# A second column page for the pair jobs, wider spaced taps, diagonal zeroing and a thinner filler in the scan

## The chip, the cores and the metric

The kernel runs on one core of one Trainium2 chip. Its time is the device time of one execution in microseconds (us); a kernel's time is the median of its runs. The engines are TensorE (PE, matmuls, with PEld for its weight loads), VectorE (DVE), ScalarE (ACT), GpSimd (POOL) and SyncE (SP), which here only issues transfers. POOL issues transfers too, among them those that add what they bring to what lies in the target.

## The reference

One layer of a hybrid encoder over 1024 positions of width 1024, in float32. Cut to what matters here:

```python
h  = rmsnorm(x)
P  = h @ W_in          # columns for: GLU of the convolution, q, v, z_fwd, z_bwd, out gate, gA, gB
A  = pointwise(swish(layernorm(dwconv31(glu(P)))))          # depthwise, 31 taps, 512 columns
B  = out_proj(norm(bi_hgrn2(q, v, z_fwd, z_bwd)) * swish(og))  # gated scan, 8 heads, both directions
x  = x + W_out(sigmoid(gA) * A + sigmoid(gB) * B)
x  = x + W_down(silu(dwconv3(h2 @ W_gate)) * (h2 @ W_up))    # h2 = rmsnorm(x)
out = rmsnorm(x)
```

The scan of one head is S_t = diag(f_t) S_{t-1} + k_t v_t^T, o_t = S_t^T q_t, forward and backward.

## The kernel before

Every number is held as a high and a low part, and every product is three matmuls (`mm3`, L147 to L149: high by high, high by low, low by high). Splitting a weight page into its two parts is a cast on ACT and a subtraction on DVE (`split`, L123). PE's instructions are issued in the order of the program; on the other engines and the transfer queues the framework orders them. Work for PE is written as generators that stop at every piece of some matmuls, and a `Stream` takes so many pieces as `fill(n)` tells it, carrying fractions (and what is overdrawn) over in `owed`.

The stages, in order of time: the first norm and the GLU jobs; then 19 pair jobs for the rest of W_in's columns; then some projection jobs; then the scan of the eight heads; its tail; the output projections, the merge, the feed-forward part and the last norm.

**Pair jobs** (`pair_job`, `in_pair`). Two blocks of 128 columns are made by a scheme of seven products instead of eight, so that sums of weight quadrants are needed. One pair has 14 pieces of six matmuls. `steps` prepares the weights of a pair: a page of rows ("wr", two buffers, `raw_w`), a page of columns ("sw", one buffer, filled by two loads of 256 KB, L304 and L305), to which src1 is added; `sums` then adds the columns to the rows and the rows to themselves. `add` does an addition on DVE where `first` holds (L296), and elsewhere with a transfer that adds, issued by POOL (L300). With `first`, src1 is loaded into a row page. Then rows are split into the weights 1 and 2, after the sums into 6 and 3, the columns into 7 and 5 ("wq"), and the last quadrant into 4. `first` holds for pair 0 and from pair 12 on. `evac` combines the products on DVE (L718) and stores them.

**Convolution** (`conv_steps`). Four column tiles, each with 31 taps on DVE (L953 the first, L956 the others), one tap at a time over 1024 positions; after each tile its two halves are stored to memory (L961). Between two taps the stream of pairs is filled:

```python
for _ in conv_steps():
    s_pairs.fill(CONV_FILL)
```

The LayerNorm then loads the tiles back half by half ("cx", L978) and adds them up (L968), with pieces of the pairs between its parts.

**Scan.** For each head and each of its two halves, `scan_levels` makes four steps (h = 8, 16, 32, 64) and `scan_states` three; each level multiplies the pages qF and kG by decays on DVE (L1061). At h = 32 a PSUM bank is zeroed by one matmul of a zero page `none` with itself (L1230), and `blocks` (L1207) writes the 32x32 and 64x64 blocks off the diagonal into it. At h = 64 the whole bank is copied to S_t, and then the 32x32 blocks on the diagonal are overwritten from D_t. After each of the 112 steps `between(FILL)` gives the stream `dense` (projections of what is left, pieces of six 128x512 matmuls) its FILL pieces, then a step of the next half's preparation, then one piece of the last head's outputs (`pending`).

**Tail** (after the loop). The last head's outputs (`outputs`: L1314, L1316, L1333, L1340) are stepped by hand between fills of `dense`, with the rest of `dense` drained at the end.

Of the kernel before, what the change touches and what calls it, by code (L numbers as in the profile page):

```python
# [10 lines left out]
F32 = mybir.dt.float32  # L11
# [5 lines left out]
AX = mybir.AxisListType  # L17

P = 128
FILL = 1.3  # L20
CONV_FILL = 1.6
NPAIRS = 19
LN_FILL = 6
LN_LAST = 12
# [6 lines left out]
H = 512  # L31
# [15 lines left out]
def tile_hybrid_encoder(  # L47
# [22 lines left out]
    nc = tc.nc  # L70
    PSUM = bass.MemoryType.PSUM
    V, A, G, T = nc.vector, nc.scalar, nc.gpsimd, nc.tensor

    S, D = x.shape[1], x.shape[2]
    ND = D // P
# [17 lines left out]
    def nm(s):  # L93
        uid[0] += 1
        return f"{s}_{uid[0]}"
# [36 lines left out]
    def raw_w(src, nk):  # L132
        t = mp.tile([P, nk, P], F32, tag="wr", name=nm("wr"), bufs=2)
        nc.sync.dma_start(t, src)
        return t
# [142 lines left out]

        return prep, run

    def pair_job(src0, src1, nk, acts, wpool, pool, evac, su=4, first=False, late=False, now=False, direct=False):

        def steps(w):
            def both(src, alt, late=late):  # L290
                hi, lo = split(w_page(2 * nk, alt), w_page(2 * nk, alt), src, V, late)
                return [(hi[:, :nk], lo[:, :nk]), (hi[:, nk:], lo[:, nk:])]

            def add(o, a):
                if first:
                    V.tensor_tensor(o, o, a, op=ALU.add)  # L296
                elif direct:
                    pin(V.tensor_tensor(o, o, a, op=ALU.add))
                else:
                    G.dma_start(o, a, accum_op=ALU.add)  # L300

            rows = raw_w(src0, 2 * nk)
            col = wpool.tile([P, 2 * nk, P], F32, tag="sw", name=nm("sw"), bufs=1)
            nc.sync.dma_start(col[:, :nk], src0[:, :nk])  # L304
            nc.sync.dma_start(col[:, nk:], src1[:, :nk])  # L305
            if not direct:
                add(col, raw_w(src1, 2 * nk) if first else src1)
            def sums():
                add(rows[:, :nk], col[:, nk:])
                add(rows[:, nk:], rows[:, :nk])  # L310

            def quadrant():
                a22 = pool.tile([P, nk, P], F32, tag="w4", name=nm("w4"), bufs=1)
                nc.sync.dma_start(a22, src1[:, nk:])
                return a22

            if now:
                w[1], w[2] = both(rows, None, False)
                sums()
                yield 0  # L320
                w[6], w[3] = both(rows, None, False)
                yield 1
                a22 = quadrant()
                yield 2
                w[7], w[5] = both(col, pool)
                yield 4
            elif direct:
                yield 2
                other = raw_w(src1, 2 * nk)
                yield 2  # L330
                w[1], w[2] = both(rows, None)
                a22 = quadrant()
                yield 6
                add(col, other)
                sums()
                yield 1
                w[6], w[3] = both(rows, None)
                yield 1
                w[7], w[5] = both(col, pool)
                yield 4  # L340
            else:
                yield 4
                w[1], w[2] = both(rows, None)
                sums()
                a22 = quadrant()
                yield 6
                w[7], w[5] = both(col, pool)
                yield 3
                w[6], w[3] = both(rows, None)
                yield 3  # L350
            one = w_page(2 * nk, pool)
            w[4] = split(one[:, :nk], one[:, nk:], a22, V, late)

        def prep():
            w = Weights(steps)
            return w if late else w.all()

        def run(w):
            def product(i, acc, fresh=True):
                for k in range(nk):  # L360
                    mm3(acc, w[i], acts(i)[k], k, fresh and k == 0, k == nk - 1, not fresh)
                    if k % 2 == 1 or k == nk - 1:
                        yield

            def copy(acc):
                t = page(pool, "su", su)
                A.copy(t, acc)  # L367
                return t

            row, b2, col = bank("mm"), bank("tr"), bank("sc")  # L370
            yield from product(1, row)
            p1 = copy(row)
            yield from product(2, b2)
            evac(0, 0, b2, p1, ALU.add)
            yield from product(6, row, False)
            u2 = copy(row)
            yield from product(7, col)
            p7 = copy(col)
            yield from product(5, row, False)
            evac(1, 1, p7, row, ALU.subtract)  # L380
            yield from product(4, col, False)
            evac(1, 0, col, u2, ALU.subtract)
            yield from product(3, row, False)
            evac(0, 1, row)

        return prep, run
# [113 lines left out]
    def in_cols(c0):  # L500
        return w_cols(w_in, 0, ND, c0)
# [206 lines left out]
    for j in range(NCW):  # L708
        g = gp0.tile([P, PAD + S + PAD], F32, tag="gl", name=nm("gl"), bufs=NCW)
# [38 lines left out]
    def in_pair(n):  # L748
        (c0, e0), (c1, e1) = todo[2 * n], todo[2 * n + 1]
        evs = (e0, e1)  # L750
        return pair_job(
            in_cols(c0),
            in_cols(c1),
            NK2,
            lambda i: ht[i],
            p1,
            p1,
            lambda e, *quadrant: evs[e](*quadrant),
            first=n == 0 or n >= 12,
        )  # L760

    gate = {}
# [200 lines left out]
    for _ in conv_steps():  # L963
        s_pairs.fill(CONV_FILL)

# [40 lines left out]
    rest = todo[2 * NPAIRS :]  # L1006
# [37 lines left out]
    dense = Stream(run_jobs(rest_jobs))  # L1044


    hp = tc.alloc_tile_pool(name="heads", bufs=1, reuse_waits="tile")
    NB = H // 8
    DE = hp.tile([P, 2, 2, H], F32, name="DE")
    dg = hp.tile([P, 4, 32], F32, name="dg")  # L1050
    none = hp.tile([P, H], mybir.dt.bfloat16, name="none")
    E0, D0 = 0, 2 * H
    for o in (E0 + 3, D0 + 3):
        G.memset(view(DE, o, [[8, 2 * NB]]), 1.0)
# [101 lines left out]
    def scan_levels(base, S_t, Tt):  # L1156
# [62 lines left out]
        b = bank("sc")  # L1219
        inside(b)  # L1220
        for h in (8, 16, 32, 64):
            n, nb = H // (2 * h), H // h
            if h < 32:
                if h == 16:
                    b = bank("ob")
                level(b, h)
            else:
                if h == 32:
                    b = bank("sc")
                    T.matmul(b, none[:, :P], none, start=True, stop=True)  # L1230
                blocks(b, h)
            tt(pairs(kG, h), pairs(kG, h), view(tb, 1, [[2, n], [nb - 1, 2], [0, h]]))
            tt(pairs(qF, h), pairs(qF, h), view(tb, nb + 1, [[2, n], [nb - 1, 2], [0, h]]))
            if h < 64:
                tn = hp.tile([P, 3, NB], F32, tag="tb", name=nm("tb"), bufs=3)
                k = 3
                to = view(tn, 0, [[n, 3], [1, n]])
            else:
                k = 2
                to = view(Tt, 0, [[4, 2], [1, n]])  # L1240
            tt(to, view(tb, 0, [[nb, k], [2, n]]), view(tb, 1, [[nb, k], [2, n]]))
            tb = tn
            if h == 8:
                A.copy(D_t, near(slot(b, 0)))
                V.copy_predicated(D_t, over(m_f), near(slot(b, 1)))
                for o, m in ((D_t, m_b), (dg, m_d)):
                    V.copy_predicated(o, over(m), near(slot(b, 2)))
            elif h == 16:
                V.copy_predicated(D_t, over(m_16), near(slot(b, 0)))
                V.tensor_tensor(D_t, D_t, dg, op=ALU.add)  # L1250
            elif h == 64:
                A.copy(S_t, c4(b))
                for g in range(0, P, 32):
                    A.copy(S_t[g : g + 32, :, g : g + 32], D_t[g : g + 32])
            yield
# [131 lines left out]
    pending = Stream(iter(()))  # L1387
    for h in range(NH):
# [4 lines left out]
        for half in range(2):  # L1393
# [13 lines left out]
            for n, _ in enumerate(scan_levels(base, S_t, Tt[:, half])):  # L1407
                if n == 2:
                    b = bank("tr")
# [3 lines left out]
                    A.copy(v.rearrange("p c e -> p (c e)"), b)  # L1413
                between(FILL)
            qF, kG = base[0], base[1]
            for _ in scan_states(i, kG, v, Tt, Sf, Sb):
                between(FILL)
            kept.append((S_t, v, qF))
            cur = ahead
        pending = Stream(outputs(h, kept, Tt, Sf, Sb))  # L1420

    left = 8 * len(rest) + 4 * ND - dense.count
    pending.fill(1)
    dense.fill(left - 20)
    pending.fill(1)
    dense.fill(4)
    pending.fill(2)
    dense.fill(4)
    pending.fill(2)
    dense.fill(4)  # L1430
    bm_loads(0)
    pending.fill(1)
    dense.fill(8)
    dense.drain()
    bm_loads(1)
    pending.drain()
# [64 lines left out]
    class Later:  # L1501


        pool = None
# [314 lines left out]
```

## Time and profile before

| | us |
|---|---|
| runs | 1784.37, 1776.78, 1784.13 |
| median | 1784.13 |
| the profiled execution | 1784.03 |
| its span in the trace | 1782.3 |
| busy in the span: PE, DVE, ACT, POOL | 1730.3, 1257.5, 773.8, 153.7 |
| mean granted clock of PE | 0.993 |

The durations below come from the profiled execution. Its own time is 1.7 us above its span, which lies around the span at both ends. A view by windows gives busy time and count of each engine in a stretch of the span. A view of waits groups an engine's idle time by the instruction that came next and by what released it, with the total, the number and the longest. A timeline has the start, the duration, the engine, the line, what it writes and reads, and in brackets the idle time before and its releaser. A PE row's duration runs longer than the distance to the next start, because matmuls overlap.

### The profile page before, as it was taken

Reading aid. Unit: us, or ns where it says so; the run is one execution under the profiler, and the core shown is the slowest. Engines: PE = TensorE matmul, PEld = TensorE weight load, DVE = VectorE, ACT = ScalarE, POOL = GpSimd, SP = SyncE. Lnnn points to the kernel's source line nnn. Section 1 sums busy time; section 2 is a strip of 40 time slices with the busy share of each in tenths; the row PEclk is TensorE's granted clock in tenths of the full one; section 3 lists DMA queues with packets and bytes.
Section 4 is the critical chain, followed back from the end, with each engine's and each line's share of the span. In section 5 each row is a group of like instructions: output and inputs, shape, how many; then the busy total and the mean of one; then the engine's idle time right before and its main releaser. Section 6 shows DMA issues by size and latency. Waiting matters only on the chain.

```text
span 1782.3 us, 27603 instructions
## 1 busy us (share of the span) xinstructions
PE 1730.3 (97%) x10614; PEld 1415.1 (79%) x10614; DVE 1257.5 (71%) x1892; ACT 773.8 (43%) x1486; POOL 153.7 (9%) x168
## 2 busy tenths in 40 slices
PE   8999999999999999999999999999999999999997
PEld 6878787888877777778878888778888888888885
DVE  5599999747679999999545567667667667444455
ACT  7343433334455656565551344344344344422123
POOL 2201111000000000000000002011111111000000
PEclk9999999999999999999999999999999999999998
DMA  8657787746663333435367665567767666534233
GB/s 286 216 154 179 189 185 183 197 152 207 195 190 109 117 119 120 131 102 189 126 209 223 189 207 182 149 147 149 153 150 155 144 150 136 159 103 127 76 91 136
DMA packets 321258, 284.29 MB, mean 160 GB/s; under 512 B 14942, under 2 KB 242022, under 8 KB 321126
## 3 DMA queue, kind: packets, MB, share of 16 engines
q1 hardware_dynamic: 279958, 250.01, 44.4%
q0 software_dynamic: 41168, 32.51, 12.8%
q8 instruction: 83, 1.36, 0.3%
q14 instruction: 49, 0.40, 0.1%
HBM read 189.40 MB, written 76.81 MB: 149 GB/s over the span
## 4 chain that ended last, share of the span: by engine, by line
PE 65%; DVE 16%; DMA 7%; issue 6%; ACT 4%; POOL 1%; SPq 0%; POOLq 0%; DVEq 0%; ACTq 0%
PE mm L147 16%; PE mm L148 16%; PE mm L149 16%; PE sc L147 3%; PE sc L149 3%; PE sc L148 3%; DVE acc L956 3%; DMA sw<-in_w_in_dram 3%; DVE kG L1061 2%; DVE wp L123 2%; DVE qF L1061 2%; DVE DE L1061 1%; PE tr L149 1%; PE tr L147 1%; PE tr L148 1%
## 5 line engine op out<-in xcount | busy, mean ns | idle before, releaser
L147 PE MATMUL mm<-hx,wp 128*128 128x512 f32 x1144 | 462.5, 404 | 9.9 <-DVE ev L718 4.7
L149 PE MATMUL mm<-hx,wp 128*128 128x512 f32 x1144 | 449.5, 393 | 1.4 <-DVE wp L123 1.4
L148 PE MATMUL mm<-hx,wp 128*128 128x512 f32 x1144 | 448.9, 392 | 0.0
L123 ACT CAST wp<-wr 128x1024 fp32r<-128x1024 f32 (+2 forms) x171 | 162.1, 949 | 352.9 <-PE mm L148 227.4
L147 PEld LDWEIGHTS mm<-hx,wp 128*128 128x128 f32 x1144 | 216.6, 189 | 57.0 <-DVE ev L718 7.6
L149 PEld LDWEIGHTS mm<-hx,wp 128*128 128x128 f32 x1144 | 216.3, 189 | 49.5 <-DVE wp L123 2.5
L123 DVE TENSOR_TENSOR wp<-wr,wp 128x1024 fp32r<-128x1024 f32 (+2 forms) x169 | 185.8, 1100 | 92.0 <-ACT wp L123 80.1
L148 PEld LDWEIGHTS mm<-hx,wp 128*128 128x128 f32 x1144 | 216.7, 189 | 41.1 <-issue 0.2
L956 DVE SCALAR_TENSOR_TENSOR acc<-gl,v_b,acc 128x1024 f32<-128x1024 f32 x120 | 149.0, 1277 | 0.5
L1670 DVE TENSOR_TENSOR xr<-mm,xr 128x512 f32<-128x512 f32 x48 | 33.2, 691 | 72.9 <-PE mm L149 72.9
L367 ACT COPY su<-mm 128x512 f32<-128x512 f32 x82 | 47.4, 578 | 56.2 <-PE mm L149 55.2
L123 ACT CAST wq<-sw 128x1024 fp32r<-128x1024 f32 x41 | 43.1, 1050 | 63.8 <-PE mm L148 29.8
L1519 DVE SCALAR_TENSOR_TENSOR tm<-gp,v_a,tm 128x512 f32<-128x512 f32 x88 | 65.9, 749 | 2.0
L147 PE MATMUL mm<-hy,wp 128*128 128x512 f32 x164 | 64.7, 395 | 2.0 <-ACT su L367 2.0
L147 PE MATMUL sc<-hy,wq 128*128 128x512 f32 x164 | 64.6, 394 | 0.0
L148 PE MATMUL mm<-hy,wp 128*128 128x512 f32 x164 | 64.3, 392 | 0.0
L149 PE MATMUL sc<-hy,wq 128*128 128x512 f32 x164 | 64.2, 391 | 0.0
L147 PE MATMUL tr<-hx,wp 128*128 128x512 f32 x164 | 63.9, 390 | 0.0
L149 PE MATMUL tr<-hx,wp 128*128 128x512 f32 x164 | 63.8, 389 | 0.0
L148 PE MATMUL tr<-hx,wp 128*128 128x512 f32 x164 | 63.8, 389 | 0.0
L148 PE MATMUL sc<-hy,wq 128*128 128x512 f32 x164 | 63.8, 389 | 0.0
L149 PE MATMUL mm<-hy,wp 128*128 128x512 f32 x164 | 63.7, 389 | 0.0
(362 smaller groups left out, 3413.8 us busy)
## 6 DMA issues: line engine op xcount, KB each, us to landing
wr<-in_w_in_dram SPq DMA_DIRECT2D x56, 512.0 KB, 4.3
wr<-in_ffn_w_up_dram SPq DMA_DIRECT2D x24, 512.0 KB, 6.1
sw<-in_ffn_w_up_dram SPq DMA_DIRECT2D x44, 256.0 KB, 3.3
d_g<-ft SPq DMA_DIRECT2D x44, 256.0 KB, 3.3
sw<-in_ffn_w_up_dram POOLq DMA_DIRECT2D x20, 512.0 KB, 8.6
sw<-in_w_in_dram SPq DMA_DIRECT2D x38, 256.0 KB, 3.2
d_z<-ev SPq DMA_DIRECT2D x32, 256.0 KB, 3.8
zi<-d_z SPq DMA_DIRECT2D x32, 256.0 KB, 2.6
```

The source lines that it names most:

```text
L123: parts = A.copy(hi, src), eng.tensor_tensor(lo, src, hi.bitcast(F32), op=ALU.subtract)
L147: T.matmul(acc, whi[:, k, :], ahi, start=first, stop=False, skip_group_check=again)
L148: T.matmul(acc, whi[:, k, :], alo, start=False, stop=False, skip_group_check=again)
L149: T.matmul(acc, wlo[:, k, :], ahi, start=False, stop=last, skip_group_check=again)
L367: A.copy(t, acc)
L956: V.scalar_tensor_tensor(acc, g[:, k : k + S], tap(k), acc, op0=ALU.mult, op1=ALU.add)
L1061: V.tensor_tensor(o, a, b, op=op)
L1519: V.scalar_tensor_tensor(c, g[:, o + k : o + k + H], vec("fdw", k * NF + j), c, op0=ALU.mult, op1=ALU.add,)
L1670: V.tensor_tensor(xr[i][half], acc, xr[i][half], op=ALU.add)
```

## The change

1. FILL goes from 1.3 to 1.265 and CONV_FILL from 1.6 to 1.67.
2. The column page of a pair job in `in_pair` has two buffers. Where `first` holds, src1 is loaded by one transfer of SP into another page of the columns and no longer into a page of the rows.
3. `first` holds for pair 0 and from pair 14 on: pairs 12 and 13 get their additions from transfers of POOL.
4. `none` is a 32 columns wide zero page, and only the sixteen 32x32 blocks on the diagonal of the bank are zeroed, by one small matmul each.
5. In the tail `owed` is set to 0, and the fills are written down in TAIL as pairs of (steps of the outputs, pieces of `dense`). After it come the load of the first output weights, a step, the rest of `dense`, the load of the second, and the rest of the outputs.

```diff
-FILL = 1.3
-CONV_FILL = 1.6
+FILL = 1.265
+TAIL = ((1, 2), (1, 1), (2, 4), (2, 3))
+CONV_FILL = 1.67
...
             rows = raw_w(src0, 2 * nk)
-            col = wpool.tile([P, 2 * nk, P], F32, tag="sw", name=nm("sw"), bufs=1)
+
+            def column_page():
+                return wpool.tile([P, 2 * nk, P], F32, tag="sw", name=nm("sw"), bufs=columns)
+
+            col = column_page()
             nc.sync.dma_start(col[:, :nk], src0[:, :nk])
             nc.sync.dma_start(col[:, nk:], src1[:, :nk])
-            if not direct:
-                add(col, raw_w(src1, 2 * nk) if first else src1)
+            if first:
+                other = column_page()
+                nc.sync.dma_start(other, src1)
+                add(col, other)
+            elif not direct:
+                add(col, src1)
...
-            first=n == 0 or n >= 12,
+            first=n == 0 or n >= 14,
+            columns=2,
...
-    none = hp.tile([P, H], mybir.dt.bfloat16, name="none")
+    none = hp.tile([P, 32], mybir.dt.bfloat16, name="none")
...
                 if h == 32:
                     b = bank("sc")
-                    T.matmul(b, none[:, :P], none, start=True, stop=True)
+                    for at, g, _ in each():
+                        T.matmul(b[g, at : at + 32], none, none, start=True, stop=True)
                 blocks(b, h)
...
-    left = 8 * len(rest) + 4 * ND - dense.count
-    pending.fill(1)
-    dense.fill(left - 20)
-    pending.fill(1)
-    dense.fill(4)
-    pending.fill(2)
-    dense.fill(4)
-    pending.fill(2)
-    dense.fill(4)
+    dense.owed = 0
+    for steps, pieces in TAIL:
+        pending.fill(steps)
+        dense.fill(pieces)
     bm_loads(0)
     pending.fill(1)
-    dense.fill(8)
     dense.drain()
     bm_loads(1)
     pending.drain()
```

More of the change, by code (lines that the diff above doesn't have):

```diff
@@ L279, in duo_job, with pair_job @@
         return prep, run
-    def pair_job(src0, src1, nk, acts, wpool, pool, evac, su=4, first=False, late=False, now=False, direct=False):
+    def pair_job(src0, src1, nk, acts, wpool, pool, evac, su=4, first=False, late=False, now=False, direct=False, columns=1):
         def steps(w):
```

## The prediction

> **What bounds the kernel now.** I read the page's busy rows first, then the busy time stretch by stretch, then what each engine waited for in the stretches that the change touches, and last the timelines around those waits. Over the whole span TensorE (PE) is the busy engine:
>
> ```profile
> PE 1730.3 (97%) x10614; PEld 1415.1 (79%) x10614; DVE 1257.5 (71%) x1892; ACT 773.8 (43%) x1486; POOL 153.7 (9%) x168
> ```
>
> So at most 1782.3 − 1730.3 = 52 us of PE idle time could be won, and the rest only by giving PE less work. The share is an average, though. The stretches are, in order: the last GLU jobs (79.5–115.3), the pair jobs beside the convolution's taps (115.3–332.6, cut at 292 where the LayerNorm begins), the pair jobs alone (to 491.6), the scan loop (522.3–886.3) and its tail (to 914.2). The columns are start:end, length, and busy time and count of each engine:
>
> ```profile
> core 0: us, PE busy (x) PEld busy (x) DVE busy (x) ACT busy (x) POOL busy (x), PEclk, DMA share, GB/s
> 79.50:115.30 35.80, 32.95 (x143) 26.30 (x141) 35.37 (x45) 13.76 (x21) 0.75 (x5) 1.00 0.48 144
> 115.30:292.00 176.70, 173.41 (x756) 141.27 (x757) 171.19 (x183) 71.39 (x102) 30.11 (x27) 1.00 0.79 180
> 292.00:332.60 40.60, 37.17 (x157) 29.93 (x155) 36.55 (x35) 11.47 (x16) 6.65 (x6) 0.96 0.77 183
> 332.60:491.60 159.00, 158.79 (x699) 129.96 (x700) 94.34 (x126) 66.12 (x101) 4.57 (x8) 1.00 0.60 190
> 522.30:886.30 364.00, 347.95 (x4515) 284.39 (x4515) 323.89 (x669) 210.95 (x522) 13.74 (x14) 1.00 0.39 125
> 886.30:914.20 27.90, 23.44 (x114) 19.03 (x112) 8.29 (x15) 15.38 (x41) 1.83 (x2) 0.88 0.46 144
> ```
>
> Three readings. From 79.5 to 332.6 VectorE (DVE) is full: it is idle 0.43 + 5.51 + 4.05 = 10.0 us of 253.1, and the PE idles there too (9.6 us). From 332.6 the pairs are PE's alone (idle 0.2 us of 159): nothing to win there, and 158.79 / 699 = 0.227 us is the pace of one 128x512 matmul. In the scan loop neither is full: PE idles 16.05 us, DVE 40.1. After 914.2 I find every engine's order unchanged by the change, so nothing is booked there. The profiled execution took 1784.03 us, 0.10 under the median of the three runs, so the sum is made on 1784.03. A difference of 0.5% (8.9 us) is about what a measurement of this kernel can tell from none.
>
> **Pairs: the wider spaced taps.** DVE's waits between 79.5 and 332.6 (total, times, longest) and PE's largest there:
>
> ```profile
> DVE wp L123 <- ACT wp L123: 5.0, 6, 2.5
> DVE tm L968 <- DMA cx<-d_cv: 3.4, 1, 3.4
> PE mm L147 <- DVE ev L718: 4.5, 4, 3.3
> ```
>
> CONV_FILL says how many pieces of a pair job go between two taps. In the order of DVE's instructions the steady state does not change at all: a pair has 14 pieces and still gets 11 taps. What does change is the ends: the first pair gets 6 taps ahead of it where it had 10, and the LayerNorm's first sum (L968) stands behind 14.0 us of DVE work after the second column's last tap, counted along the new order with the present durations, where it stands behind 9.4 now. That sum waits for the convolution's trip to memory and back:
>
> ```profile
> 293.54 0.87 SPq L961 DMA_DIRECT2D d_cv<-acc  x2
> 297.89 1.67 SPq L978 DMA_DIRECT2D cx<-d_cv  x2
> ...
> 306.29 0.69 DVE L968 TENSOR_TENSOR tm<-cx 128x512 f32<-128x512 f32 x1 [3.39 <-DMA cx<-d_cv]
> 306.90 3.92 DVE L956 SCALAR_TENSOR_TENSOR acc<-gl,v_b,acc 128x1024 f32<-128x1024 f32 x3
> 310.74 0.68 DVE L718 TENSOR_TENSOR ev<-su,mm 128x512 f32<-128x512 f32 x1
> ```
>
> The trip takes 306.29 − 293.54 = 12.75 us. With 14.0 us of work ahead of the sum the 3.39 us wait goes. What is late next is the same eviction (L718) that PE waits for, which is behind DVE's work only. So this is −3.4.
>
> **Pairs: the second column page.** The six waits of the row splits (L123) end one chain: the column page "sw" comes free when its split is done, is loaded again, gets src1 added by a transfer that POOL issues, and only then are the two row additions (also POOL's) issued; the split then waits for ScalarE's cast, which waits for the second addition:
>
> ```profile
> 178.84 1.58 POOL L300 DMA_DIRECT2D sw<-in_w_in_dram  x1 [4.81 <-DMA sw<-in_w_in_dram]
> 188.92 0.89 POOL L300 DMA_DIRECT2D wr<-sw  x1 [8.49 <-DVE kscale L1067]
> ...
> 184.71 1.21 DVE L123 TENSOR_TENSOR wp<-wr,wp 128x1024 fp32r<-128x1024 f32 x1
> ...
> 178.29 1.05 ACT L123 CAST wp<-wr 128x1024 fp32r<-128x1024 f32 x1 [3.70 <-DMA wr<-wr]
> ```
>
> The row addition is issued at 188.92, though the split of the same rows is done at 184.71 + 1.21 = 185.92; between them it waits for the column's addition, issued 10.1 us before. With two pages that addition belongs to the pair before and stands one pair earlier in POOL's queue, so the row additions could start 3.0 us earlier, more than the longest wait of 2.5. But the addition of the pair after next now stands ahead of them on that same queue, at about the time it has now, so part of its transfer lies beside theirs. I take 3.0 of the 5.0 us; the ends are 0 and 5.0.
>
> Pairs 12 and 13 add their columns on POOL's queue instead of DVE (6 DVE instructions less, after 332.6 for the most part, where DVE is idle 64.7 us: 0). Pair 0 still adds on DVE, from a second column page of 512 KB that SP loads behind the first:
>
> ```profile
> 69.83 0.58 SPq L304 DMA_DIRECT2D sw<-in_w_in_dram  x1
> ...
> 112.92 1.22 DVE L296 TENSOR_TENSOR sw<-sw,wr 128x1024 f32<-128x1024 f32 x1
> ```
>
> In the new order this addition stands at the head of the stretch, near 79.5, 10 us after the first page is issued. How late the second lands the trace can't show; the longest wait for a transfer around the splits is ACT's 3.70 above, so 0 to +3.7. I take a quarter, +0.9, because 10 us is nearly the 10.1 that a transfer of that size took on POOL's queue. Together the stage gives −3.4 − 3.0 + 0.9 = −5.5. The ends: −10.0 (all of DVE's idle time) and −3.4 + 3.7 = +0.3.
>
> **Scan: the zeroing.** One 128x512 matmul of zeros becomes 16 of 32x32, sixteen times (8 heads, 2 halves):
>
> ```profile
> 527.43 0.39 PE L1230 MATMUL sc<-none 128*128 128x512 bf16 x1
> 527.75 0.46 PE L1207 MATMUL sc<-qF,kG 128*32 128x32 f32 x32
> ...
> L1193 PE MATMUL sc<-Qh,Kh 128*32 128x32 f32 x1024 | 12.2, 199 | 0.0
> ```
>
> Now it takes 527.75 − 527.43 = 0.32 us. The group of the same small shape takes 12.2 / 1024 = 11.9 ns each, so 16 take 0.19: 0.13 less, times 16 is −2.1. In 5 of the 16 halves PE waits right behind it (L1207 <- qF, below), and there it gives nothing: 11/16 of 2.1 is −1.4. TensorE: Matmul & The Clock Gate, of the Trainium skill, says in "Wait — 56ns, not 53.3ns?" that matmuls never start less than about 25 ns apart, however small: 16 would be 0.40 us and this term +1.3 in place of −2.1; the row of 1024 at 11.9 ns does not agree.
>
> **Scan: the filler.** FILL 1.3 → 1.265 takes the loop's pieces from 145 to 141 (of 112 steps 24 lose one and 20 gain one); a piece is 6 matmuls, 1.36 us, so 5.45 us of PE work leave the loop and stand in the tail. PE's waits in the loop:
>
> ```profile
> PE ob L1181 <- DVE qF L1061: 5.7, 8, 0.9
> PE tr L1264 <- DVE kG L1061: 4.7, 6, 1.8
> PE sc L1207 <- DVE qF L1061: 3.2, 5, 1.2
> ...
> 673.81 0.66 PE L1264 MATMUL tr<-ident,kG 128*128 128x128 f32 x4 [1.76 <-DVE kG L1061]
> ```
>
> Where a step loses a piece, its gain is 1.36 only if DVE's chain of that step has as much in hand; where it hasn't, PE waits instead. No step with a wait now loses a piece; five with a wait gain one. So between all of it (−5.45) and none (0, each piece replaced by a wait) I take half, −2.7, because the loop's idle time on DVE (40.1 us) leaves room but each chain of steps is serial. The loop gives −4.1; ends −7.6 and 0.
>
> **Tail.** Ten pieces now stand in 27.9 us with 27.90 − 23.44 = 4.46 us of PE idle, most of it one wait, after which the matmuls run at about half pace:
>
> ```profile
> 898.79 0.48 PE L1340 MATMUL tr<-ident,tm 128*128 128x128 f32 x1 [2.09 <-ACT tm L1333]
> 899.61 1.06 PE L1340 MATMUL tr<-ident,tm 128*128 128x128 f32 x3 [0.34 <-ACT tm L1333]
> 900.32 0.77 PE L147 MATMUL mm<-hx,wp 128*128 128x512 f32 x1
> ...
> 905.58 0.43 PE L147 MATMUL mm<-hx,wp 128*128 128x512 f32 x1
> ```
>
> From 900.32 to 905.58 are 12 matmuls, 5.26 us where 12 × 0.227 = 2.7: 2.5 lost. The fills before it leave nothing to put there: the budget had run negative, so that three fills of 4 yielded 2 pieces. After the change 2, 1, 4 and 3 pieces stand before the four waits and 4 behind. Added work 5.45, waits −4.46, slow pace −2.5: −1.5. If 1 us of waits stays and with it nothing else, −0.5; if the slow pace stays too, +2.0.
>
> By "What's actually happening" on the same page of the Trainium skill the clock falls after an idle window of about 3.4 us; the slow pace here came after 2.09 + 0.34 us, so this case's row does not agree. By that rule no step of the loop could slow, and rival 3 would have no price.
>
> **Sum:** −5.5 − 4.1 − 1.5 = −11.1, so 1784.03 − 11.1 = 1772.9. All gains at their ends: −10.0 − 7.6 − 1.5 = −19.1, 1764.9. The forecast's own range is 1765 to 1778.
>
> **Rivals.**
> 1. *The waits come back.* The row additions stay where they are, since the transfer now ahead of them on POOL's queue takes the same time, and each piece that leaves the loop becomes a wait for DVE. What stays is the LayerNorm's wait and the tail: −3.4 − 1.5 = −4.9, 1779.1. For it: the windows show DVE full in the first stage. Against it: 40.1 us of DVE idle time in the loop. With pair 0's +3.7 and the slow pace of the tail kept (+2.5) it ends at 1785.3.
> 2. *The small matmuls don't run at the group's pace.* They are bf16 where the group's are f32, and each stands with a load of its own. At twice 11.9 ns they take 0.38 us against 0.32: 16 × 0.06 = +1.0 in place of −1.4, 1775.3. Against it: the 1024 in the group carry a load each as well.
> 3. *Slower: the thinned loop lets the clock drop.* The tail's row shows half pace after 2.4 us of waiting; the loop's longest wait, 1.76, was not followed by it. If the steps that lose a piece (24, three in each head) make one wait per head longer than somewhere between 1.76 and 2.43, each costs 2.5 us: 8 × 2.5 = +20, with pairs and tail (−7.0) 1797. It decides from the third such wait on (3 × 2.5 against 7.0). Against it: a lost piece uncovers 1.36 us, and steps that lose one have no wait now.
> 4. *It doesn't do what it says.* The pairs are held by something else than the page (only the first of the gains is in the order itself), and nothing moves: 1784.
>
> **How the numbers follow.** Forecast 0.64, of which 0.56 lies under 1775.1 (0.5% faster) and 0.08 above; rival 1 0.17; rival 2 0.06; rival 3 0.10; rival 4 0.03. Rival 1 is likelier than the others because it needs only what the first stage's windows show. Faster 0.56; same 0.08 + 0.17 + 0.06 + 0.03 = 0.34; slower 0.10. The predicted time is the forecast's, 1773. The range runs from 1763 (1764.9, less 2 because one of the three runs of before lay 7 us under the others) to 1785 (rival 1's end); it leaves out rival 3, and about 0.05 of the forecast below.
>
> **What would show it.** In the profile after: DVE's waits between 79.5 and 332.6 with no L968 entry (3.4) and the row splits' entry near 2; the stretch from 79.5 to the last tap some 5 us shorter; the small zeroing matmuls some 12 ns apart; the loop some 4 us shorter with its PE idle time near 20; the tail some 1.5 us shorter, with more pieces, no wait over 1 us and no half pace. Wrong would be: row additions still issued 3 us behind their split, a slow clock inside the loop, or the loop as long as now with more PE idle time.

## The result, and the profile after

The changed kernel took 1770.28 us (median of 5 runs, 1769.65 to 1772.84) against 1784.13 before (5 runs, 1776.78 to 1784.73). The ratio is 0.9935, with a 95% interval of 0.9914 to 0.9956. The forecast was 1773, and the range 1763 to 1785. The profiled execution after took 1770.28 us, with a span of 1768.5.

The first view is by stretches, with the same marks in both kernels, counted in PE instructions: from where the first tap starts in before (in the changed kernel it starts at 88.2) to the prediction's cut at 292, from there to the end of the pairs, the scan loop up to its last state product, and the tail from there to the output projections. The prediction's cuts lay a little later in the loop (886.3), so the lengths of loop and tail differ from the ones shown there. First before, then after (length, then busy time of PE, PEld, DVE, ACT, POOL, then the granted clock):

```profile
core 0: us, PE busy (x) PEld busy (x) DVE busy (x) ACT busy (x) POOL busy (x), PEclk, DMA share, GB/s
79.48:292.00 212.52, 206.38 (x899) 167.58 (x898) 206.56 (x227) 85.17 (x122) 30.86 (x32) 1.00 0.74 174
292.00:491.43 199.43, 195.79 (x855) 159.72 (x854) 130.73 (x159) 77.45 (x116) 11.23 (x14) 0.99 0.63 189
522.35:884.04 361.69, 345.64 (x4502) 282.36 (x4502) 322.17 (x664) 210.31 (x520) 13.74 (x14) 1.00 0.39 124
884.04:914.18 30.14, 25.68 (x129) 21.03 (x127) 9.94 (x19) 16.01 (x43) 1.83 (x2) 0.89 0.49 149
```

```profile
79.36:284.87 205.51, 203.72 (x899) 168.12 (x898) 202.78 (x226) 86.79 (x122) 32.44 (x33) 1.00 0.79 185
284.87:481.63 196.76, 194.32 (x854) 158.59 (x853) 129.13 (x155) 76.55 (x116) 15.95 (x19) 1.00 0.66 191
512.78:872.75 359.97, 339.71 (x4717) 278.83 (x4717) 321.98 (x663) 208.53 (x517) 13.81 (x14) 1.00 0.38 123
872.75:900.35 27.60, 27.46 (x153) 23.33 (x151) 8.68 (x18) 15.41 (x43) 1.83 (x2) 1.00 0.52 167
```

The pairs lost 411.95 − 402.27 = 9.7 us, the loop 1.7, the tail 2.5. Everything else is within 0.3. In the first part of the pairs PE idled 6.1 us of 212.5 and now 1.8 of 205.5; DVE idled 6.0 and now 2.7, so both are nearly full. In the loop PE's busy time fell by 5.9 but its idle time grew from 16.05 to 20.26, so two thirds of the removed work came back as waiting. In the tail PE now idles 0.14 us, at full clock.

That what follows the tail is equally long is no sign that nothing changed there. The first 400 matmuls behind the tail take 93.6 us where they took 90.8: the output projections now wait for the splits of their weights (three rows below), where before PE waits nowhere. Before loses as much later, in code that the change does not touch: there it waits 3.56 us (last row) where the change waits 1.30, and then runs 11 matmuls at half pace (starts 0.43 us apart in place of 0.23) where the change runs none.

```profile
901.61 0.50 PE L150 MATMUL mm<-hx,wp 128*128 128x512 f32 x1 [0.53 <-DVE wp L124]
...
923.98 0.50 PE L148 MATMUL mm<-hx,wp 128*128 128x512 f32 x1 [0.73 <-ACT wp L124]
...
925.24 0.50 PE L150 MATMUL mm<-hx,wp 128*128 128x512 f32 x1 [0.53 <-DVE wp L124]
```

```profile
1159.48 0.80 PE L147 MATMUL mm<-hx,wp 128*128 128x512 f32 x1 [3.56 <-ACT su L367]
```

Of DVE's waits from 79.5 to 320 none on the LayerNorm's sum (L978 now, at 305.85) is left, and 1.0 of the row splits' (total, times, longest; the last line is PE's, its only one there). From 320 to the last tap, which ends at 329.9, a row split waits 0.4 us more and PE 1.65, so that 1.4 us stand against the row splits' 5.0 before:

```profile
DVE tm L402 <- DMA su<-d_h: 1.7, 2, 1.2
DVE gl L784 <- PE mm L150: 1.2, 1, 1.2
DVE acc L963 <- DMA d_cv<-acc: 1.0, 1, 1.0
DVE wp L124 <- ACT wp L124: 1.0, 2, 0.7
PE mm L148 <- ACT tm L778: 1.8, 1, 1.8
```

The row additions now follow the split that they need. The split below ends at 159.52 + 1.21 = 160.73 and the addition is issued at 161.03, where before it came 3.0 us after its split:

```profile
159.52 1.21 DVE L124 TENSOR_TENSOR wp<-wr,wp 128x1024 fp32r<-128x1024 f32 x1
161.03 0.88 POOL L301 DMA_DIRECT2D wr<-sw  x1 [5.30 <-DVE wp L124]
```

### The profile page after: what moved, and what is told of

It is laid out like the page before. It is cut to its first block, busy times and chain, and to the rows that moved or that the text cites. A ratio compares the mean times of both kernels' runs of the same rounds, so it can differ in the third digit from the quotient of the medians.

```text
span 1768.5 us, 28121 instructions
## 1 busy us (share of the span) xinstructions
PE 1721.4 (97%) x10854; PEld 1410.2 (80%) x10854; DVE 1251.3 (71%) x1886; ACT 774.1 (44%) x1486; POOL 160.3 (9%) x174
## 4 chain that ended last, share of the span: by engine, by line
PE 70%; DVE 14%; DMA 6%; ACT 5%; issue 3%; POOL 1%; SPq 0%; POOLq 0%; ACTq 0%; DVEq 0%
PE mm L148 16%; PE mm L150 16%; PE mm L149 16%; PE sc L148 4%; PE sc L150 4%; PE sc L149 4%; DVE DE L1071 2%; PE tr L148 2%; PE tr L150 2%; PE tr L149 2%; DVE qF L1071 2%; DVE kG L1071 2%; DVE wp L124 2%; DMA wr<-in_w_in_dram 1%; DVE Kh L1074 1%
```

## The experiments

Times are medians; each ratio is against runs of before on the same chip, with its 95% interval. Where runs of before were taken with the experiments their medians were 1781.55 to 1781.71, 2.4 to 2.6 below the five runs above, so the ratios are the better measure. A stretch comes from the one profiled execution of its kernel; "pairs" is the sum of the first two stretches above, "loop" and "tail" are the other two. A stretch moves by up to 3 us without an edit to it: two kernels that have the pairs of before, `zero` and `fill_tail`, show 412.05 and 414.9 for "the pairs" (before: 411.95). So differences of 1 to 3 us between single executions are not taken as shown.

**The column page alone.** Two pages, src1 of a first pair in the second; the rest as before.

```diff
-                add(col, raw_w(src1, 2 * nk) if first else src1)
+            if first:
+                other = column_page()
...
             first=n == 0 or n >= 12,
+            columns=2,
```

> Only the second column page (two buffers for the columns, src1 of a first pair loaded there; additions on DVE still for pair 0 and from pair 12 on), all else as before. If the row splits wait because the column page is freed late, their 5.0 us of DVE waiting between the first tap and the end of the taps fall under 2 and the LayerNorm's 3.4 us wait (L968 of before) stays: the stretch from the first tap to the end of the pairs 4 to 6 us shorter than the 412.1 of before, some 1779 us. Rival, the transfer that now stands ahead on POOL's queue takes the place of the old wait: stretch within 1 us of 412, 1784 us. Rival, the page wins only together with the spacing, since the time is handed to the LayerNorm's wait: row splits' waits go, that wait grows to 6 or more.

Measured: 1777.88, ratio 0.9978 (0.9968 to 0.9989); pairs 409.2. The row splits' waits fell to 1.4 us, but PE still had two long waits, one of 2.43 us at 97.50 and the one below, and the sum waits:

```profile
DVE tm L977 <- DMA cx<-d_cv: 2.7, 1, 2.7
DVE wp L123 <- ACT wp L123: 1.4, 1, 1.4
...
172.52 0.50 PE L147 MATMUL mm<-hx,wp 128*128 128x512 f32 x1 [2.37 <-DVE ev L726]
172.86 0.40 PE L148 MATMUL mm<-hx,wp 128*128 128x512 f32 x1
173.10 0.59 PE L149 MATMUL mm<-hx,wp 128*128 128x512 f32 x1
173.49 0.63 PE L147 MATMUL mm<-hx,wp 128*128 128x512 f32 x1
```

After each of them PE ran 8 matmuls at half pace. So the page works as described and gains a part.

**The wider spacing alone.**

```diff
-CONV_FILL = 1.6
+CONV_FILL = 1.67
```

> Only CONV_FILL 1.67, all else as before. If the wider spacing is worth the LayerNorm's wait alone: that wait (3.4 us) gone, the row splits' waits near 5.0 as before, the stretch from the first tap to the end of the pairs 3 to 4 us shorter than 412.1, some 1780.5 us. Rival, the spacing also loosens the row splits' chain, since the first pair starts earlier against the taps: their waits fall too and the stretch is 6 us or more shorter. Rival, no effect: what DVE gains there PE gives back after the taps: 1784 us.

Measured: 1783.44, ratio 1.0009 (0.9999 to 1.0018); pairs 411.5. Nothing is gained:

```profile
DVE wp L123 <- ACT wp L123: 4.8, 6, 1.5
DVE tm L968 <- DMA cx<-d_cv: 3.2, 1, 3.2
```

The reason stands in the order of DVE's instructions. With the spacing alone it has exactly as many taps ahead of every eviction as before, and the sum stands where it stood. The order of each kernel, counted at 1.2 us for a 1024-wide and 0.6 for a 512-wide instruction:

| kernel | taps ahead of the 1st, 4th, 8th and 32nd eviction of the pairs | DVE work from the column's last tap to the sum |
|---|---|---|
| before, and spacing alone | 10, 20, 36, 123 | 9.0 us |
| page alone | 6, 17, 35, 122 | 7.8 us |
| page and spacing, whole change | 6, 17, 33, 120 | 13.2 us |

**Page and spacing together.** Both diffs above.

> Second column page and CONV_FILL 1.67 together (additions on DVE from pair 12 on, scan as before). Alone the page made the stretch from the first tap to the end of the pairs 2.8 us shorter (409.2 for 411.95) and kept a 2.7 us wait of the LayerNorm's sum; the spacing alone left that wait at 3.2 and the stretch at 411.5. In the order of DVE the sum stands behind 9.0, 7.8 and 9.0 us of work after the column's last tap in before, page and spacing, and behind 13.2 with both. Theory: only the two together put the sum late enough; the wait is 0 and the stretch 8 to 10 us shorter than before, some 1772 to 1774 us. Rival: the two add (-2.8 and -0.4), and what the whole change gained beyond that comes from pairs 12 and 13 or from chance in one execution: some 1778 us.

Measured: 1772.48, ratio 0.9951 (0.9936 to 0.9966); pairs 402.1. DVE's waits and PE's, all of them:

```profile
DVE tm L401 <- DMA su<-d_h: 2.3, 1, 2.3
DVE acc L962 <- DMA d_cv<-acc: 1.4, 1, 1.4
DVE gl L783 <- PE mm L149: 1.2, 1, 1.2
DVE sw L296 <- DMA sw<-in_w_in_dram: 0.4, 1, 0.4
PE mm L147 <- ACT tm L777: 2.1, 1, 2.1
PE mm L147 <- DVE ev L726: 0.9, 1, 0.9
```

Neither the sum nor a row split waits. The two together took 9.9 us off the pairs, where each alone took 2.7 and 0.5. The times say the same beyond their intervals: 0.5% together, where the page alone gives 0.2% and the spacing alone nothing.

**All of the change to the pairs,** with the additions of pairs 12 and 13 as transfers, and the scan as before.

```diff
-            first=n == 0 or n >= 12,
+            first=n == 0 or n >= 14,
```

> All of the change to the pairs (page, spacing, additions of pairs 12 and 13 by transfers), scan as before. Theory: pairs 12 and 13 run in the stretch that PE bounds, so their 6 DVE instructions are worth nothing: within 1 us of the page and spacing together, and the scan gives the rest of the whole change (4 us), some 1773 us. Rival: the instructions lie on the DVE that is late at the end of the taps, 3 to 5 us better than the page and spacing.

Measured: 1774.13, ratio 0.9961 (0.9949 to 0.9973); pairs 403.2. So pairs 12 and 13 are worth nothing that can be told, as the prediction had it.

**The page alone, with the sum begun at other tiles.** The spacing stays at 1.6.

```diff
-        mean = bank("ob")
-        T.matmul(mean, ones_m, total(xs, tmp()), start=True, stop=True)
+        mean = bank("ob")
+        T.matmul(mean, ones_m, total([xs[3], xs[0], xs[1], xs[2]], tmp()), start=True, stop=True)
```

> Second column page alone, spacing as before, and the LayerNorm's sum of four tiles begins with the tiles that end it now (3, 0, 1, 2 in place of 0, 1, 2, 3): in the order of DVE it then stands behind the last tap. If the superadditive part of the page and the spacing is this one wait, it is gone here without the spacing (no L977 wait of 2.7 us), and the stretch from the first tap to the end of the pairs is 2.5 to 7 us shorter than the page alone's 409.2, some 1772 to 1776 us. Rival: the spacing itself is needed (the taps' end comes too late against the pairs at 1.6): within 1 us of the page alone, 1778 us.

Measured: 1776.44, ratio 0.9967 (0.9953 to 0.9982); pairs 406.8, between the theory and its rival. The sum's wait is gone, but in the stretch this is left, DVE's wait first, then PE's, then the eviction and the matmul of its longest:

```profile
DVE wp L123 <- ACT wp L123: 2.0, 1, 2.0
PE mm L147 <- DVE ev L726: 3.8, 2, 3.3
...
170.25 0.70 DVE L726 TENSOR_TENSOR ev<-su,mm 128x512 f32<-128x512 f32 x1
171.00 0.80 PE L147 MATMUL mm<-hx,wp 128*128 128x512 f32 x1 [3.31 <-DVE ev L726]
```

By single executions, the sum's place accounts for 2.4 of the 7.2 us between the page alone and the page with the spacing; that is within what a stretch moves by itself, and the intervals of the two ratios (0.9978 and 0.9967) overlap, so this share isn't shown. The rest is argued from the order of the taps, and no run moved these taps alone: at 1.6 the order takes back two taps between the 7th and the 8th eviction (28 to 35, where it is 28 to 33 with the spacing), and the 8th is the eviction at 170.25 for which PE waits here, and for which it waited at 172.52 in the page alone.

**The whole change at a spacing of 1.75.** Taps ahead of each eviction as in the whole change, within one; the sum behind 6.6 us of work.

```diff
-CONV_FILL = 1.67
+CONV_FILL = 1.75
```

> The whole change with CONV_FILL 1.75 in place of 1.67. In the order of DVE the number of taps ahead of each pair's evictions stays that of the whole change (within one), but the LayerNorm's first sum stands behind 6.6 us of work after the column's last tap, not 13.2. Theory: that place alone is worth the wait, so L978 waits 5 to 7 us again (12.75 less 6.6), PE waits some 3 to 5 us behind it, and the time is 3 to 6 us above the whole change. Rival, the taps' number ahead of the evictions is what counts and DVE has slack there: the sum waits, but the stretch is within 1 us of 402.3.

Measured: 1780.77, ratio 0.9998 (0.9986 to 1.0010): the whole gain is gone, 9.7 us against the whole change on the same chip. Two waits of DVE, then PE at the start of the scan loop:

```profile
303.36 0.69 DVE L978 TENSOR_TENSOR tm<-cx 128x512 f32<-128x512 f32 x1 [2.36 <-DMA cx<-d_cv]
341.71 0.69 DVE L980 TENSOR_TENSOR tm<-tm,cx 128x512 f32<-128x512 f32 x1 [5.40 <-DMA cx<-d_cv]
...
520.72 0.66 PE L1191 MATMUL sc<-qF,A 128*32 128x32 f32 x32 [3.68 <-ACT A L1189]
521.90 0.63 PE L149 MATMUL mm<-hx,wp 128*128 128x512 f32 x1
```

The sum waits, but 2.36 us and not the 5 to 7 expected, and the pairs grew only to 404.4. The larger part lies where neither theory looked: the sum's later terms wait 5.4 us for the last column, and the scan loop is 367.8 us long against 360.0, 3.68 of it one wait for the first head's preparation, with 8 matmuls at half pace in the loop. The sum's wait was short because the trip to memory was: 303.36 − 294.14 = 9.2 us from the store's issue to the sum, where it was 12.75 in before. The preparation is late from its start: its first loads of `zi` are issued at 495.96, behind a store of the pairs at 493.39, and in the whole change at 483.56. Why the order of these transfers changed, and whether DVE's later waits have a part in it, wasn't tried. So this run doesn't isolate the sum's place.

**The zeroing alone.**

```diff
-                    T.matmul(b, none[:, :P], none, start=True, stop=True)
+                    for at, g, _ in each():
+                        T.matmul(b[g, at : at + 32], none, none, start=True, stop=True)
```

> Only the diagonal zeroing by sixteen 32x32 matmuls, all else as before. By the prediction's price (0.32 us to 0.19 each time) the scan loop is 1.4 to 2.1 us shorter than its 361.7, some 1782 us. Rival, read in the profile of the change: the 0.32 us is mostly what any small matmul waits behind a 128x512 one (there the first small zeroing starts 0.32 us after the matmul ahead of it, where the large zeroing started 0.23 after it), so that from the matmul ahead to the first block it is 0.51 against 0.55: 16 times 0.04 = 0.6 us, not to be told from nothing in the time, but in these distances.

Measured: 1785.25, ratio 1.0019 (1.0006 to 1.0031); loop 362.5. What a zeroing costs is read from three starts: the matmul ahead, the zeroing, the first block. The first row is of before, whose next two stand in the prediction; the others are two of the whole change's sixteen:

```profile
527.20 0.39 PE L149 MATMUL mm<-hx,wp 128*128 128x512 f32 x1
```

```profile
537.35 0.40 PE L150 MATMUL mm<-hx,wp 128*128 128x512 f32 x1
537.68 0.28 PE L1241 MATMUL sc<-none 128*32 128x32 bf16 x16
538.70 0.46 PE L1217 MATMUL sc<-qF,kG 128*32 128x32 f32 x32 [0.74 <-DVE qF L1071]
...
560.59 0.39 PE L1325 MATMUL ob<-Sb,qF 128*128 128x128 f32 x2
560.91 0.28 PE L1241 MATMUL sc<-none 128*32 128x32 bf16 x16
561.02 0.47 PE L1217 MATMUL sc<-qF,kG 128*32 128x32 f32 x32
```

Before, the zeroing starts 0.23 us after the matmul ahead and the block 0.32 after that: 0.55. Now nine of the sixteen stand behind a 128x512 matmul and start 0.32 to 0.33 us after it, and the block mostly 0.11 to 0.12 after that: 0.32 + 0.11 = 0.43. The other seven stand behind a 128x128 matmul, as in the second group of rows: 0.21 + 0.11, where before has 0.11 + 0.31. The sixteen small ones are indeed fast, 0.11 / 16 = 7 ns apart, but the step from 128-wide to 32-wide work costs 0.1 us, which was paid behind the zeroing and is now paid ahead of it. So some 0.11 is saved each time, 1.8 us in all. "It is 0.51 against 0.55" was read from a row that isn't typical. In `zero` PE's waits in the loop came to 17.7 us against 15.65 before, and in the whole change to 19.75 against 17.7 with the large zeroing (next run): in both pairs 2 us more, so the saving became waiting, as in the row at 538.70.

**The whole change with the large zeroing.**

> The whole change but the zeroing, which is the one large matmul again. In the profile the small form saves PE 0.11 us each time (0.31 ahead and 0.11 of its own, against 0.23 and 0.31), 1.8 us in all, but where it was tried alone the loop's waits grew by 2.0 us and its length by 0.8. Theory: DVE's chain takes up what PE saves there, so within 1 us of the whole change. Rival, the small form costs time (alone it measured 1.0019 of before): this one 2 to 4 us faster than the whole change, and the best version. Rival, the prediction's: 1.4 us slower.

Measured: 1769.76, ratio 0.9930 (0.9916 to 0.9944). The whole change run beside it:

> The whole change once more, on the chip of the three runs that follow, to compare them with: 1769.5 to 1773, the stretch from the first tap to the end of the pairs near 402.3, no half pace of more than single matmuls.

It took 1771.09, ratio 0.9936 (0.9922 to 0.9950), pairs 403.3, loop 361.5 with 5 matmuls at half pace after a wait of 1.99 us and PE idle for 20.3 us. In the taps' stretch of this execution the row splits wait 3.3 us, and PE runs 7 matmuls at half pace from 323.95 on, after a wait of 2.31. With the large zeroing the loop is 359.3. The two times can't be told apart: the zeroing is worth nothing in the whole change. Why alone it measured slower by 0.2% stays open. No version was clearly better than the change.

**The filler and the tail alone.**

```diff
-FILL = 1.3
+FILL = 1.265
+TAIL = ((1, 2), (1, 1), (2, 4), (2, 3))
```

> Only FILL 1.265 and the tail's new order, all else as before. If PE sets the loop's pace where pieces leave, the loop is 2.7 us or more shorter than 361.7, and the tail 1.5 to 2.8 shorter than 30.1: some 1779. Rival, DVE sets the loop's pace and each piece that leaves becomes a wait: loop within 1 us of 361.7 with PE idle time of 20 or more where it was 16, the tail alone gains, 2 to 3 us: some 1781.5.

Measured: 1781.84, ratio 0.9995 (0.9983 to 1.0006). In the trace the loop is 359.8 (−1.9) and the tail 27.7 (−2.4), both within 0.2 of the whole change, but the pairs of that execution stand at 414.9, and in the time nothing shows. By its trace loop and tail give 4.3 us, but the first 400 matmuls behind the tail take 92.6 us against 90.8, so 1.8 of it is lost again at once. The whole change lies below all of the pairs' edits (0.9935 and 0.9936 against 0.9961), by some 4.5 us with intervals that just touch. So that the scan's edits gain something is likely; how much isn't shown.

**The filler alone,** with the fills of the tail as before.

> Only FILL 1.265, with the tail as before, pairs and zeroing as before. Theory: the thinner filler pays only with the new order of the tail: the loop is 1 to 2 us shorter than 361.7, but the 4 pieces add 5.4 us to the tail, where the old fills let them stand after the waits, not under them: tail and loop together 3 to 4 us longer than before, some 1785 us. Rival, the thinner loop gains all that the tail loses: 1781.5, as before.

Measured: 1782.47, ratio 1.0003 (0.9994 to 1.0012). Loop and tail:

```profile
522.97:882.66 359.69, 340.98 (x4478) 277.97 (x4477) 321.54 (x664) 209.68 (x517) 13.80 (x14) 1.00 0.38 123
882.66:913.13 30.47, 27.89 (x153) 23.56 (x151) 9.20 (x19) 16.21 (x44) 1.83 (x2) 1.00 0.49 164
```

The loop's 2.0 us are the filler's own. The tail took four pieces more (5.45 us) and grew by 0.3: it idles 2.6 us in place of 4.5, and its clock stayed at 1.00. So the pieces themselves cover waits, and the new order only the rest, 2.8 us. But the old tail does not always run at half pace: in the run with the sum begun at other tiles (`page_sum`) it has the same wait (2.10 us) and no half pace behind it, and takes 27.6 us, as long as the new tail.

**The whole change with FILL 1.3.**

> The whole change, but FILL 1.3 as before: four pieces stay in the loop and are missing at the end of the tail. Where the loop is DVE's, a piece costs nothing in the loop and 1.36 us in the tail: the loop grows by 1 to 2 us and the tail shrinks by up to 5.4, so 3 to 4 us faster than the whole change, some 1767 us. Rival: PE sets the loop's pace: the loop grows by what the tail shrinks, 1770 us. Rival: the missing pieces uncover the first output projections' weights (their split was 0.53 us late already): a wait of 4 us or a half pace there, 1772 us or more.

Measured: 1773.90, ratio 0.9957 (0.9941 to 0.9973). The tail is 21.7, 5.9 us shorter, but the loop is 363.8 and the first output projections wait (loop first, then tail, then the 21 us behind it):

```profile
513.45:877.28 363.83, 346.18 (x4742) 284.69 (x4741) 323.03 (x664) 210.58 (x520) 13.87 (x14) 1.00 0.39 124
877.28:898.95 21.67, 21.67 (x128) 18.95 (x126) 5.85 (x14) 13.10 (x39) 1.83 (x2) 1.00 0.43 138
898.95:920.00 21.05, 17.47 (x66) 12.78 (x64) 14.10 (x21) 9.87 (x16) 0.00 (x0) 0.92 0.83 269
...
906.86 0.50 PE L148 MATMUL mm<-hx,wp 128*128 128x512 f32 x1 [2.25 <-ACT hx L124]
```

The third theory agrees: without four pieces ahead of them the projections idle 3.6 us (0.5 in the whole change) and run 8 matmuls at half pace. After 400 matmuls behind the tail this kernel is 3.8 us behind the whole change, which is what the four pieces cover there. By the end it is 4.9; the other 1.1 come from half pace at 1151 us, in code that no edit touches. In the time alone the difference isn't clear, since the intervals of 0.9957 and 0.9936 overlap.

## Why the prediction was right, step by step

The time was right (1773 for 1770.28; −11.1 us for −13.8 against the profiled execution), the likeliest case came in, and in the first profile the signs called for were there: no L968 entry, the row splits' waits under 2 us, no half pace in the tail. In the second profile of the same kernel they were not all: the row splits wait 3.3 us, and two of the signs that the prediction named as wrong came, a slow clock in the loop and a loop as long as now (361.5 to 361.7) with more idle time. By stages the sum was off in both directions: the pairs gave 9.7 for 5.5, the loop 1.7 for 4.1, the tail 2.5 for 1.5. That the total is within 3 us is in part luck.

- **What bounds the kernel.** Half right. The taps' stretch was DVE's, with 10.0 us to win until the last tap. Of these 5.5 were won (4.5 are left), and the last tap ends 5.1 us earlier, at 329.9 for 335.0, as the prediction said. But the pairs became 9.7 us shorter. The other 4.6 lie behind the last tap, where the prediction saw "nothing to win": PE idled 3.4 us in place of 9.6 in the taps' stretch and lost none of it to half pace, so it had some 24 more matmuls done at the last tap, and 151.7 us of pairs left in place of 156.4. That PE's own waiting is worth time was the term put at nothing.
- **The spacing, −3.4.** The mechanism, the sum's place against the trip to memory, was there, but the step put it on the wrong edit. It read the sum's place in the order of the whole change and credited the spacing, which alone changes no place at all. The 3.4 us needs page and spacing.
- **The page, −3.0, with +0.9 for pair 0.** Mis-sized: the additions start behind their split as predicted, the transfer now ahead of them on POOL's queue did not hold them back, and with the spacing 3.6 of the 5.0 us went in the first execution of the whole change, 1.7 in the second and all of it in page and spacing. Pair 0's addition doesn't wait in any run, so the +0.9 was nothing. (The 0.4 us of L296 in page and spacing, and 1.7 in the run with the other sum, are pair 12's addition, at 325.79 and 331.96.) A further gain wasn't seen: less DVE work ahead of the evictions, and with it no wait of PE after which it ran at half pace there (8 matmuls in before, none after; 7 in the second execution).
- **Zeroing, −1.4.** Wrong in its price and its place. The 0.32 us was taken as the zeroing's own, but 0.1 of it is what the change of shape costs either way; 0.11 is saved each time, and DVE's chain takes it up. Of the five waits counted as standing behind a zeroing only two do (0.62 and 0.33 us); the others are the same line at other steps. Rival 2's doubt of the pace was unfounded: 7 ns apart. The 25 ns of the Trainium skill (TensorE: Matmul & The Clock Gate, "Wait — 56ns, not 53.3ns?") don't hold in this row either.
- **Filler, −2.7.** Measured −1.7 to −2.0 in three traces and −0.2 in the second of the whole change, so more of it became waits than the half that was taken: rival 1's mechanism, in part. PE's idle time in the loop near 20 was right. The prediction booked nothing behind the tail because no engine's order changes there. The waits for the splits of the output weights came all the same, 2.8 us in the first 400 matmuls; that less work ahead of them uncovers them agrees with the run with FILL 1.3, where four pieces less cost 3.8 us more.
- **Tail, −1.5.** Measured −2.5, against a tail of before that ran at half pace. The half pace cost more than the 2.5 us counted, since transposes ahead of it ran slow as well. Against the tail of `page_sum`, without half pace, the gain would be nothing.
- **Rival 3.** No half pace over single matmuls in the loop of the first profile of the whole change, though its longest wait was 1.94 us; in the second, 5 matmuls after a wait of 1.99. So its mechanism occurs, once and not in every head, and costs some 1 us. Its point "between 1.76 and 2.43" isn't a threshold, as the last section shows.

## What to carry to other kernels

When a scheduler orders an engine, compute the order for each edit alone before crediting one with what the order of the whole shows: here two edits were worth 0.5 and 2.7 us apart and 9.9 together. A stretch that is as long as before may hold a loss and a gain, so compare it piece by piece. Where two engines are nearly equally full (171 and 173 us of 177 here, before), what counts is not their sum but which work stands ahead of the instruction that the other waits for. And a short instruction's cost is the distance between its neighbours' starts with it and without it, not its own row.

## What the hardware showed that was not expected

Waits of the same length were followed by half pace in some places and not in others. The first row, of the whole change with FILL 1.3, has a wait of 1.86 us and half pace from 666.61 on, 0.43 us from start to start. The last two are one place in two executions of the whole change: half pace follows the wait of 1.99 us and not the one of 1.94:

```profile
665.53 0.86 PE L1275 MATMUL tr<-ident,kG 128*128 128x128 f32 x4 [1.86 <-DVE kG L1071]
666.04 0.78 PE L148 MATMUL mm<-hx,wp 128*128 128x512 f32 x1
666.61 0.63 PE L149 MATMUL mm<-hx,wp 128*128 128x512 f32 x1
```

```profile
620.42 0.86 PE L1275 MATMUL tr<-ident,kG 128*128 128x128 f32 x4 [1.99 <-DVE kG L1071]
```

```profile
618.42 0.66 PE L1275 MATMUL tr<-ident,kG 128*128 128x128 f32 x4 [1.94 <-DVE kG L1071]
```

By start-to-start distances, and single matmuls left out, before had 30 matmuls at half pace after the first 60 us, the whole change none in its first execution and 12 in its second. The wait of 3.56 us in before, shown with the result, stands at a place that no edit touches, and all fourteen traces have it: the six waits of 2.95 us or more were followed by half pace, and of the eight shorter ones only one, of 1.81. TensorE: Matmul & The Clock Gate of the Trainium skill says in "What's actually happening" that the window in which idleness is judged runs freely; by that the same wait could be caught or not, which agrees with the rows, though no run tests it. Its length of about 3.4 us doesn't agree with a drop after 1.86. And the step from a 128-wide matmul to 32-wide ones took 0.1 us more than to another 128-wide one (0.33 against 0.23), a price that is paid once for a group of small matmuls however many it holds.
